# Half of the memory tokens loaded into free activation tiles behind the first key weight, and the delta rule's masked ratios made by VectorE

## The chip, the cores and the metric

The kernel runs on one core of a Trainium2 chip. The metric is the time of one execution on the device in microseconds: 2902.29 us, the median of three runs (2901.53 to 2903.21).

## The reference

One layer of a streaming encoder on 512 tokens of width 2048, in float32. The input is normalised and projected by one matrix; its columns feed a gated delta rule (8 heads of 128) and an RWKV-7 mixer (16 heads of 64). Their outputs are projected and added, then follow cross attention into 256 memory tokens, a squared-ReLU MLP and a last norm.

```python
h  = x
y  = rmsnorm(h, norm_mix) @ w_in                       # 512 x 2048 by 2048 x ~7500
h += concat[GDN(y_gdn), RWKV7(y_rwkv)] @ w_out
mn = rmsnorm(mem, norm_mem)                            # 256 memory tokens
k, v = mn @ wk, mn @ wv ; q = rmsnorm(h, norm_xattn) @ wq
h += softmax(q k^T / sqrt(512)) v @ wo                 # 4 heads of 512
h += square(relu(rmsnorm(h, norm_mlp) @ w_up)) @ w_down
out = rmsnorm(h, norm_final)
```

In the delta rule a chunk's matrix is masked by position and scaled by the ratio of decays:

```python
gamma = where(i >= j, exp(G[i] - G[j]), 0)
M     = where(i > j, (beta k)_i . k_j * gamma, 0)      # solved as (M + I) X = rhs
```

## The kernel before

Activations lie with the width on the 128 partitions, so the input is 16 tiles of 128 x 512. A float32 product is made of two-part numbers: `split_` writes a rounded high half on ScalarE (`whi`, `xhi`) and the rest on VectorE (`wlo`, `xlo`), and TensorE adds high by high, low by high and high by low. A projection block of 128 output columns (`py`) takes 16 x 3 matmuls of 128 x 512; its weight comes as two halves of 128 x 1024 (512 KB). There are 59 such blocks (NIN), the stage of the first 911 us.

Between these matmuls stands the work of the mixers. Per head pair j the function `rwkv` and per head h the function `gdn` form small matrices, whose 16 x 16 diagonal blocks are inverted by `inverse_blocks` on GpSimd (tiles `sr` for RWKV, `sgi`, `sgj` for the delta rule): the matrix is stored to DRAM (`ndri`, `ndgi`), read back as blocks, inverted in some thirty small operations, stored again (`bg16T`, `bg8T` and so on) and read into the tiles `r`, `E`, `gk`, `gqn`. `inverse_levels` then joins the blocks by matmuls (`ri7x`, `ri7w`, `ri7u`, and `gi7x` and so on; the digit is the pair or head). In `gdn` the norm of the keys is a sum of squares over partitions, done as a matmul (`gn`, inputs `sumh`, `suml`), and the products of keys are `pkk`. The tile `gE` holds the ratios gamma, `gEs` the same with the strict mask and a minus sign.

Behind the projections come the key stage and the query stage: `kp` multiplies the memory by the key weights, `kq` multiplies the keys by the query weights. In `kp` a weight half serves 8 matmuls of 128 x 512 (high half of the weight against both halves of the memory, side by side in a tile `mhl`) and 8 of 128 x 256. The order of halves is (block 0, first half), (1, first), (0, second), (1, second), then block by block.

The order of the work is not that of the code. Each function is a generator (a chain) that yields one operation at a time; `run` takes, again and again, the chain whose next operation can start first by the planner's own account (`start`, `cost`: fixed prices for each engine and 2.9 us and more for a DMA's landing), with a rank added. The operation is then recorded in `issue`, so that nearly all rows of the profile have its line, 256. Engines run what they were given in order, and so does the queue of DMA issues on SyncE (SP): a DMA that waits holds all behind it. The planner knows an engine's speed alone, nothing of two engines in each other's way. A chain also waits inside the planner for its turn: an operation for a busy GpSimd holds the chain's later operations back until the plan's clock has come to it.

`loader` works off the list `wq` of loads through three buffers (`wraw`), each taken when the buffer's last content was split: weights ("w"), and the memory in four parts of 512 KB, once for its sums of squares ("s") and once for its values ("m"). `memory` splits a part into four tiles `mhl`, which lie in the places (tag "act", 32 tiles) of the input tiles `xhi`, `xlo`; it waits until the last projection has used them (events "x"). `presums`, low in rank, fills free time with sums of blocks of the down projection (tiles `ds`, stored as `sd`). The later stages (`vp`, `vo`, output and MLP) use the same places again.

Of the kernel before, what the change touches and what calls it, by code (L numbers as in the profile page):

```python
# [17 lines left out]
P = 128  # L18
T = 512
M = 256  # L20
# [53 lines left out]
def build(tc, I, out):  # L74
# [23 lines left out]
    def col(name, i=0):  # L98
        o, w = PRM[name]
        return prm[:, o + i:o + i + 1]  # L100
# [92 lines left out]
    class Lane:  # L193
# [6 lines left out]
        def __getattr__(self, nm):  # L200
# [3 lines left out]
                return self.key, nm, getattr(self.eng, nm), a, k, out, aps, self.slack  # L204
            return op

    SL, SM = Lane(nc.sync, "SP", wait=6000.0), Lane(nc.sync, "SP", margin=8000.0)
    DV, AC, GS, TE, SY = (Lane(e, k) for e, k in ((V, "DVE"), (S, "ACT"), (GP, "POOL"), (PE, "PE"), (nc.sync, "SP")))

# [136 lines left out]
        yield TE.matmul(pt, which, hi, start=False, stop=True)  # L346
        lock.pop()

    def act_tile(nm, dt=F32R):
        return tile_of(pa, [P, 512], dt, "act", nm, 32)  # L350

    mixd = [pd.tile([P, T], F32, name=f"mixd{i}", tag=f"mixd{i}") for i in range(16)]
    KQd = [pd.tile([P, 1024], F32, name=f"kqd{i}", tag=f"kqd{i}") for i in range(16)]
# [58 lines left out]
                yield from presum(e, m, c, min(c + width, 2048), d, Lane(nc.sync, "SP", margin=5000.0), Lane(nc.sync, "SP", 0.0, 0.0))  # L412

    hk = [("w", I["wk"][n][:, h * 1024:(h + 1) * 1024]) for n, h in kpo]
    wq += [("m", m) for m in mem4[:3]] + hk[:1] + [("m", mem4[3])] + hk[1:]
    wq += [("w", I["wqT"][n][:, g * 1024:(g + 1) * 1024]) for n in range(KD) for g in range(2)]
    NKP, NKQ = 2 * NIN, 2 * NIN + 2 * KD
    raws, halves, used, whole, piece = {}, {}, set(), set(), {}
# [12 lines left out]
    def loader():  # L431
        w = nm = 0
        for i, (kind, _) in enumerate(wq):
            yield lambda: i in raws
            if kind == "w":
                if w in (2, 3):
                    hi, lo = (tile_of(pm, [P, 1024], F32R, t, f"w{t}", 1) for t in ("BK", "AR", "GA", "GB")[2 * w - 4:2 * w - 2])
                else:
                    prev = (w if w < 2 else w - 2) - NWS
                    if prev >= 0:  # L440
                        yield lambda: prev + 2 * (prev > 1) in used
                    hi, lo = halves[w] if w in piece else wsplit()
                if w in piece:
                    yield after("piece", w)
                    yield from split_(raws[i][:, 512:], hi[:, 512:], lo[:, 512:])
                else:
                    yield from split_(raws[i], hi, lo)
                    halves[w] = hi, lo
                whole.add(w)
                w += 1  # L450
            else:
                yield from (memory if kind == "m" else squares)(nm % 4, raws[i])
                nm += 1
            if NWR < i + NWR <= 2 * NWR:
                chain(late(i + NWR), 2)
            elif i + NWR < len(wq):
                yield rawload(i + NWR)
# [29 lines left out]

    def xin():
        for k in range(KD):
            hi, lo = act_tile(f"xhi{k}"), act_tile(f"xlo{k}")  # L490
            yield from split_(xr[k], hi, lo, col("norm_mix", k))
            xhi.append(hi)
            xlo.append(lo)
            if k + XA < KD:
                yield xload(k + XA)
# [70 lines left out]
    def projections():  # L566
        pts = [psb(f"py{n}") for n in range(2)]
        yield from gemm_(pts, xhi, xlo, 0)
        for n in range(2):
            chain(evict(n, pts[n]), 0)  # L570
        for n in range(2, NIN):
            if n == NSQ[3] + 3:
                yield after("macc")
                pt = psb("pms", "mm", 2)
                mc = ybuf[macc[0]]
                yield TE.matmul(pt[:, 0:M], ones, mc[:, 0:M], start=True, stop=False)
                yield TE.matmul(pt[:, 0:M], ones, mc[:, M:2 * M], start=False, stop=True)
                chain(memnorm(pt, mc[:, M:2 * M]), 1)
            if n >= 4:
                yield after("py", n - 2)  # L580
            pt = psb(f"py{n}", "mm", 2)
            yield from gemm_([pt], xhi, xlo, 2 * n, left="x" if n == NIN - 1 else None)
            chain(evict(n, pt), 0)
        yield after("py", NIN - 2)
        kpt = {}
        for i, (n, h) in enumerate(kpo):
            if h == 0:
                yield after("kp", n - 2) if n >= 2 else after("py", NIN - 1)
                kpt[n] = psb(f"kp{n}", "mm", 2)
            pt = kpt[n]  # L590
            yield half(NKP + i)
            wh, wl = halves[NKP + i]
            for part in (0, 1) if h == 0 else (1, 0):
                for k in range(8 * h, 8 * h + 8):
                    yield lambda: len(mhl) > k
                    if part == 0:
                        yield TE.matmul(pt, wh[:, k % 8 * P:k % 8 * P + P], mhl[k], start=k == 0, stop=k == KD - 1)
                    else:
                        yield TE.matmul(pt[:, 0:M], wl[:, k % 8 * P:k % 8 * P + P], mhl[k][:, 0:M], start=False, stop=False)
            used.add(NKP + i)  # L600
            if h == 0:
                continue
            t = act_tile(f"khl{n}")
            khl.append(t)
            chain(kevict(n, pt, t[:, 0:M], t[:, M:2 * M]), 0)
        for i in range(2 * KD):
            n, g = i // 2, i % 2
            if i == 0:
                yield after("inverted", 7)
            yield after("kp", KD - 2 + i) if i < 2 else after("kq", i - 2)  # L610
            yield half(NKQ + i)
            wh, wl = halves[NKQ + i]
            pts = [psb(f"kq{n}_{g}_{hh}", ("mm", "mg")[hh], 2) for hh in range(2)]
            for z in range(8):
                yield TE.matmul(pts[z // 4], wh[:, z * P:z * P + P], khl[g * 8 + z], start=z % 4 == 0, stop=False)
            for z in range(8):
                yield TE.matmul(pts[z // 4][:, 0:M], wl[:, z * P:z * P + P], khl[g * 8 + z][:, 0:M],
                                start=False, stop=z % 4 == 3)
            used.add(NKQ + i)
            chain(qevict(i, pts), 0)  # L620
# [463 lines left out]
    def gdn(h):  # L1084
# [45 lines left out]
            yield DV.scalar_tensor_tensor(out=E[:, cs], in0=E[:, cs], scalar=RT[:, c, 0, h:h + 1],  # L1130
                                          in1=K("mbias"), op0=ALU.subtract, op1=ALU.min)
        yield AC.activation(E, E, AF.Exp)
        Es = tl("gEs")
        yield GS.tensor_tensor(out=c3(Es), in0=c3(E), in1=K("sneg").unsqueeze(1).broadcast_to([P, 4, P]), op=ALU.mult)
        kn = yield from normed(k_, None, "gkn", 0)
        kb = tl("gk")
        yield DV.tensor_tensor(out=kb, in0=kn, in1=B, op=ALU.mult)
# [1 line left out]
        for c in range(4):  # L1139
            cs = slice(c * P, (c + 1) * P)  # L1140
            yield TE.matmul(pkk[:, cs], kn[:, cs], kb[:, cs], start=True, stop=True)
        NTm = Es
        yield DV.tensor_tensor(out=NTm, in0=pkk, in1=Es, op=ALU.mult)

        def store(full):
            yield SY.dma_start(full[:, 0:4, :], c3(NTm)[hA, :, 0:64])
# [83 lines left out]
            chain(gdn(h + 1), 3)  # L1230


    mhl = []
    mrs = rstd[:, 0:M]
    macc = []

# [15 lines left out]
    def memory(k4, raw):  # L1252
        for i in range(4):
            k = 4 * k4 + i
            yield after("x", k // 2)
            t = act_tile(f"mhl{k}")
            yield from split_(raw[:, i * M:(i + 1) * M], t[:, 0:M], t[:, M:2 * M], col("norm_mem", k))
            mhl.append(t)

    def memnorm(pt, mw):  # L1260
        yield from rsq_(mw, pt[:, 0:M], 1.0 / 2048, b_eps6)
# [23 lines left out]
    chain(pieces(), 1)  # L1285
    chain(consts(), 3)
    chain(loader(), 2)
    chain(xin(), 1)
    chain(xsum(), 4, ("rstd",))
    chain(derived(), 3, ("derived",))  # L1290
# [1149 lines left out]
```

## Time and profile before

| what | value |
|---|---|
| median of three runs | 2902.29 us |
| the profiled execution: its time, its span | 2902.95 us, 2901.2 us |
| TensorE (PE) busy | 2868.0 us, 99% |
| VectorE (DVE), ScalarE (ACT) busy | 2333.1 us, 1569.9 us |
| GpSimd (POOL) busy | 227.0 us, all of it in the first 14 of 40 slices |
| moved by DMA | 553.01 MB, 191 GB/s on average |

A row of the timeline is start, duration, engine, line, operation, output<-inputs and tile sizes; in brackets stands the engine's idle time ahead of the row and what ended it. SPq rows are DMA issues. A row of the waits gives the waiting engine and tile, whom it waited for, the total, the number of times and the longest. Matmuls are pipelined: from one start to the next is the time that counts, the duration of one is longer. A granted clock (PEclk) of 1.00 is full speed.

### The profile page before, as it was taken

The page shows a single profiled execution, that of the slowest core. Times are in us where ns is not written, and L with a number is a line of the kernel's source. Part 1 is how long each engine was busy: PE and PEld are TensorE (multiplying, and loading weights), DVE is VectorE, ACT ScalarE, POOL GpSimd, SP SyncE. Part 2 cuts the span into 40 slices and gives each one's busy share as a digit, 9 for nine tenths or more (in the row PEclk, how much of TensorE's full clock was granted, in tenths as well). Part 3 has the DMA queues.
Part 4 walks back from the last instruction along what each step waited for, and adds up shares of the span by engine and source line. Part 5 has one row for each costly group of instructions (what it writes and reads, how often), then busy time and mean ns, then how long its engine had stood idle before and what let it go on. Part 6 is the DMA issues. An engine that isn't in the chain of part 4 may idle for free.

```text
span 2901.2 us, 49161 instructions
## 1 busy us (share of the span) xinstructions
PE 2868.0 (99%) x18794; PEld 2420.4 (83%) x18794; DVE 2333.1 (80%) x3551; ACT 1569.9 (54%) x2233; POOL 227.0 (8%) x547
## 2 busy tenths in 40 slices
PE   8999999999999999999999999999999999999998
PEld 7877877777777888879988888888888888888887
DVE  7787787787887876769956898899998878787888
ACT  6454555545655555564444656555555645454544
POOL 0213213223122100000000000000000000000000
PEclk9999999999999999999999999999999999999999
DMA  5657556556656688684423344656665878978733
GB/s 190 175 143 184 160 160 173 161 154 185 173 154 198 199 256 276 229 286 159 125 94 94 106 157 158 196 194 203 187 201 181 291 243 278 296 256 273 267 102 109
DMA packets 320924, 553.01 MB, mean 191 GB/s; under 512 B 101096, under 2 KB 188396, under 8 KB 320688
## 3 DMA queue, kind: packets, MB, share of 16 engines
q1 hardware_dynamic: 293296, 518.41, 57.9%
q10 hardware_dynamic: 27392, 31.46, 3.1%
q8 instruction: 147, 2.41, 0.3%
q14 instruction: 89, 0.73, 0.1%
HBM read 443.45 MB, written 106.31 MB: 189 GB/s over the span
## 4 chain that ended last, share of the span: by engine, by line
PE 93%; DMA 2%; DVE 2%; ACT 1%; issue 1%; ACTq 0%; SPq 0%; DVEq 0%
PE py L256 22%; PE mxu L256 12%; PE mgd L256 6%; PE mgu L256 6%; PE mxd L256 6%; PE op L122 5%; PE vp L122 3%; PE mmu L256 3%; PE sc L122 3%; PE at L122 3%; PE mmd L256 3%; PE scrd L256 3%; PE scgd L256 3%; PE kq L256 3%; PE kp L256 3%; PE vo L122 1%
## 5 line engine op out<-in xcount | busy, mean ns | idle before, releaser
L256 ACT CAST whi<-wraw 128x1024 fp32r<-128x1024 f32 (+1 forms) x366 | 383.4, 1048 | 364.2 <-PE py L256 150.4
L256 DVE TENSOR_TENSOR wlo<-wraw,whi 128x1024 fp32r<-128x1024 f32 (+1 forms) x366 | 450.5, 1231 | 101.0 <-ACT whi L256 92.2
L256 PE MATMUL py<-xhi,whi 128*128 128x512 f32 x928 | 372.6, 401 | 8.1 <-ACT xhi L256 8.1
L256 PE MATMUL py<-xhi,wlo 128*128 128x512 f32 x928 | 372.8, 402 | 0.0
L256 PE MATMUL py<-xlo,whi 128*128 128x512 f32 x928 | 372.7, 402 | 0.0
L256 ACT CAST whi<-w 128x1024 fp32r<-128x1024 f32 x176 | 185.3, 1053 | 170.3 <-PE mxd L256 35.2
L256 DVE TENSOR_TENSOR wlo<-w,whi 128x1024 fp32r<-128x1024 f32 x176 | 214.8, 1221 | 44.4 <-ACT whi L256 41.1
L256 PE MATMUL mxu<-cb,whi 128*128 128x512 f32 x1016 | 249.3, 392 | 0.0
L256 PEld LDWEIGHTS mxu<-cb,whi 128*128 128x128 f32 x1016 | 184.7, 189 | 34.3
L256 PEld LDWEIGHTS py<-xhi,whi 128*128 128x128 f32 x928 | 175.0, 189 | 42.6 <-ACT xhi L256 8.1
L256 PEld LDWEIGHTS py<-xhi,wlo 128*128 128x128 f32 x928 | 175.0, 189 | 35.5 <-issue 1.8
L256 PEld LDWEIGHTS py<-xlo,whi 128*128 128x128 f32 x928 | 174.9, 189 | 34.8 <-DVE xlo L256 0.5
L131 DVE TENSOR_TENSOR wlo<-wraw,whi 128x1024 fp32r<-128x1024 f32 x112 | 136.6, 1221 | 44.0 <-ACT whi L130 43.5
L130 ACT CAST whi<-wraw 128x1024 fp32r<-128x1024 f32 x112 | 117.6, 1051 | 85.9 <-PE op L122 29.4
L256 PE MATMUL mxu<-cb,wlo 128*128 128x256 f32 x1016 | 142.7, 283 | 0.7 <-DVE wlo L256 0.7
L256 PEld LDWEIGHTS mxu<-cb,wlo 128*128 128x128 f32 x1016 | 135.1, 191 | 6.0 <-DVE wlo L256 0.9
L256 ACT ACT_TABLE_LOAD x87 | 111.6, 1283 | 36.4 <-DVE suml_gn L256 16.5
L256 PE MATMUL mgu<-cb,whi 128*128 128x512 f32 x512 | 129.3, 394 | 0.1
L256 PE MATMUL mxd<-whi,cb 128*128 128x512 f32 x512 | 126.7, 389 | 0.7 <-DVE acc L256 0.7
L256 PE MATMUL mgd<-whi,cb 128*128 128x512 f32 x512 | 126.4, 389 | 0.0
L256 ACT CAST whi<-ws 128x1024 fp32r<-128x1024 f32 x75 | 79.0, 1053 | 72.3 <-PE mgu L256 48.2
L122 PE MATMUL op<-ob,whi 128*128 128x256 f32 (+1 forms) x752 | 115.3, 304 | 0.1
(945 smaller groups left out, 6447.2 us busy)
## 6 DMA issues: line engine op xcount, KB each, us to landing
wraw<-in_w_in SPq DMA_DIRECT2D x116, 512.0 KB, 4.6
wraw<-in_w_up SPq DMA_DIRECT2D x65, 512.0 KB, 3.6
w<-in_w_up SPq DMA_DIRECT2D x63, 512.0 KB, 4.0
ds<-in_w_dm SPq DMA_DIRECT2D x128, 205.0 KB, 4.1
sd_s<-ds SPq DMA_DIRECT2D x128, 205.0 KB, 4.7
wraw<-sd_s SPq DMA_DIRECT2D x51, 512.0 KB, 4.9
w<-sd_s SPq DMA_DIRECT2D x50, 512.0 KB, 5.5
w<-in_w_dm SPq DMA_DIRECT2D x48, 512.0 KB, 5.0
```

The costliest lines, as they stand in the source:

```text
L122: PE.matmul(o, l, r, start=start, stop=stop, skip_group_check=again)
L130: S.copy(hi, src)
L131: V.tensor_tensor(out=lo, in0=src, in1=hi.bitcast(F32), op=ALU.subtract)
L256: f(*a, **k)
```

## The change

Two things are changed, and with them the planner's order wherever it bears on them.

The memory's values. The list of loads now begins the key stage with the first key weight, then two of the four memory parts, then the other weights. The other two parts no longer go through the three buffers: the new chain `straight` loads them as four tiles `mraw` of 128 x 512 into the places of the input tiles 4 and 5, as soon as the last projection has used these, and `placed` splits them from there. For that the 32 places are kept as two groups, 28 ("act") and 4 ("acr"); later tiles take the small one where the count of tiles, in groups of four, is at group 7, 11, 19, 27 or 35. The event "direct" starts `placed` when the first two parts are at their last tile. `mhl` becomes a dictionary, and a kp matmul waits for its own tile.

The masked ratios. The product of `gE` with the mask is taken from GpSimd, where it stood ahead of the norm of the keys in the chain, and given to VectorE, behind the products of keys and right ahead of the operation that uses it.

```diff
+    SD = Lane(nc.sync, "SP", 0.0, 1500.0)
...
-    def act_tile(nm, dt=F32R):
-        return tile_of(pa, [P, 512], dt, "act", nm, 32)
+    acts = [0]
+
+    def act_tile(nm, dt=F32R, x=None):
+        few = x in (4, 5)
+        if x is None:
+            few = acts[0] // 4 in (7, 11, 19, 27, 35)
+            acts[0] += 1
+        return tile_of(pa, [P, 512], dt, "acr" if few else "act", nm, 4 if few else 28)
...
-    wq += [("m", m) for m in mem4[:3]] + hk[:1] + [("m", mem4[3])] + hk[1:]
+    wq += hk[:1] + [("m", m) for m in mem4[:2]] + hk[1:]
...
-                yield from (memory if kind == "m" else squares)(nm % 4, raws[i])
+                yield from (memory if nm >= 4 else squares)(nm % 4, raws[i])
...
-            hi, lo = act_tile(f"xhi{k}"), act_tile(f"xlo{k}")
+            hi, lo = act_tile(f"xhi{k}", x=k), act_tile(f"xlo{k}", x=k)
...
-                    yield lambda: len(mhl) > k
+                    yield lambda: k in mhl
...
-        Es = tl("gEs")
-        yield GS.tensor_tensor(out=c3(Es), in0=c3(E), in1=K("sneg").unsqueeze(1).broadcast_to([P, 4, P]), op=ALU.mult)
...
-        NTm = Es
-        yield DV.tensor_tensor(out=NTm, in0=pkk, in1=Es, op=ALU.mult)
+        NTm = tl("gEs")
+        yield DV.tensor_tensor(out=c3(NTm), in0=c3(E), in1=K("sneg").unsqueeze(1).broadcast_to([P, 4, P]), op=ALU.mult)
+        yield DV.tensor_tensor(out=NTm, in0=pkk, in1=NTm, op=ALU.mult)
...
+            if k == 7:
+                events.add(("direct",))
             yield from split_(raw[:, i * M:(i + 1) * M], t[:, 0:M], t[:, M:2 * M], col("norm_mem", k))
-            mhl.append(t)
+            mhl[k] = t
+
+    def straight():
+        for j in range(4):
+            yield after("x", 4 + j // 2)
+            t = tile_of(pa, [P, 512], F32, "acr", f"mraw{j}", 4)
+            yield SD.dma_start(t.rearrange("p (a b) -> p a b", b=M), mem4[2 + j // 2][:, j % 2 * 2:j % 2 * 2 + 2, :])
+            direct[j] = t
+
+    def placed():
+        yield after("direct")
+        for k in range(8, KD):
+            yield lambda: (k - 8) // 2 in direct and ("x", k // 2 + 2) in events
+            t, raw = act_tile(f"mhl{k}"), direct[(k - 8) // 2][:, k % 2 * M:k % 2 * M + M]
+            yield from split_(raw, t[:, 0:M], t[:, M:2 * M], col("norm_mem", k))
+            mhl[k] = t
...
+    chain(straight(), 1)
+    chain(placed(), 2)
```

The DMA queue SP at the end of the projections, before, from the store of the last RWKV inverse on (`in_wk` are key weights, `in_memT` the memory, `lg` a gate weight, `sd` and `ds` the sums of the down projection):

```order
L256 DMA bg16T<-sr_10077 64x16x16
L256 DMA bg16U<-sr_10077 64x16x16
L256 DMA lg_10354<-in_g2a 128x128
L256 DMA lg_10354<-in_g2b 32x128 x3
L256 DMA r_10299<-bg16T 64x8x64 x2
L256 DMA E_558_10300<-bg16U 64x4x64 x4
L256 DMA wraw_10395<-in_wk 128x1024
L256 DMA sd_1_s_154<-ds_55_829 128x410
L256 DMA sd_1_s_156<-ds_54_828 128x410
L256 DMA wraw_10444<-in_memT 128x1024
L256 DMA sd_1_s_155<-ds_53_827 128x410
L256 DMA wraw_10475<-in_wk 128x1024
```

The same place in the changed kernel:

```order
L257 DMA bg16T<-sr_10099 64x16x16
L257 DMA bg16U<-sr_10099 64x16x16
L257 DMA wraw_10354<-in_memT 128x1024
L257 DMA r_10357<-bg16T 64x8x64 x2
L257 DMA E_564_10358<-bg16U 64x4x64 x4
L257 DMA mraw_10417<-in_memT 128x512
L257 DMA mraw_10425<-in_memT 128x512
L257 DMA mraw_10428<-in_memT 128x512
L257 DMA mraw_10434<-in_memT 128x512
L257 DMA wraw_10402<-in_wk 128x1024
L257 DMA sd_1_s_154<-ds_55_829 128x410
L257 DMA sd_1_s_156<-ds_54_828 128x410
```

Before, the first key weight is the first load behind the reads of the inverse, and three memory parts went out ahead of the rows shown. Now the key weight shown is the second; the first stands 15 rows ahead of bg16T, right behind the read of the inverse's blocks (sr), with one memory part after it, and the second memory part and the four direct loads stand here. The read sr, which followed two stores (ndri), four loads ds, a store mixd and a memory part, follows the two stores and one ds.

TensorE in the key stage, before, where the first level of the last RWKV inverse ends (ri7u) and the second begins:

```order
L256 MATMUL ri7s_10530<-k_10406,E_558_10300 64x64 x2
L256 MATMUL ri7t_10531<-k_10406,E_558_10300 64x64 x2
L256 MATMUL ri7u_10529<-E_558_10300,k_10406 64x64 x16
L256 MATMUL ri7x_10592<-r_10299,GA_9996 64x64
L256 MATMUL ri7x_10592<-r_10299,GB_9997 64x64
L256 MATMUL ri7w_10593<-r_10299,GA_9996 64x64
```

And now:

```order
L257 MATMUL ri7s_10581<-k_10419,E_564_10358 64x64 x2
L257 MATMUL ri7t_10582<-k_10419,E_564_10358 64x64 x2
L257 MATMUL ri7u_10580<-E_564_10358,k_10419 64x64 x16
L257 MATMUL kp_10562<-mhl_10459,wlo_10507 128x256
L257 MATMUL kp_10562<-mhl_10464,wlo_10507 128x256
L257 MATMUL kp_10562<-mhl_10469,wlo_10507 128x256
```

Where the second level followed at once, 23 kp matmuls stand between, and one more ahead of pkk behind it. Ahead of the first level stand the last projection matmuls and 4 kp (before: the sum gn, which has moved into the projections, and 6 kp); between its ri7w and ri7s stand 21 kp instead of 10.

GpSimd before, at the end of an RWKV inverse in the fourth head (sr) and the start of a delta-rule inverse (sgi):

```order
L256 TENSOR_TENSOR sr_4934<-sr_4934,sr_4935 64x15
L256 COPY sr_4934<-sr_4934 64x256
L256 TENSOR_TENSOR gEs_5218<-gE_4369,cst 128x512
L256 MEMSET sgi_5328 32x256
L256 MEMSET sgi_5328 32x16
```

VectorE in the changed kernel, in the same head:

```order
L257 TENSOR_TENSOR wlo_5188<-wraw_4906,whi_5187 128x1024
L257 TENSOR_TENSOR gk_5200<-gkn_5175,gqd_4951 128x512
L257 TENSOR_TENSOR gEs_5227<-gE_4208,cst 128x512
L257 TENSOR_TENSOR gEs_5227<-pkk_5219,gEs_5227 128x512
L257 SCALAR_TENSOR_TENSOR gq_5233<-y_182,prm,gq_5233 128x512 x3
```

The mask's product has left GpSimd, whose order is otherwise the same, and stands on VectorE directly ahead of the product with pkk.

2 lines of the change are left out of this document (1 added, 1 removed).

## The prediction

> **What bounds the kernel now.** I read the page's busy times first, then the list of waits on PE, then PE in order of time where those waits fall, with the granted clock.
>
> ```profile
> span 2901.2 us, 49161 instructions
> PE 2868.0 (99%) x18794; PEld 2420.4 (83%) x18794; DVE 2333.1 (80%) x3551; ACT 1569.9 (54%) x2233; POOL 227.0 (8%) x547
> ...
> PE py L256 <- ACT xhi L256: 8.1, 1, 8.1
> PE kp L256 <- ACT whi L256: 4.4, 1, 4.4
> PE gn L256 <- DVE suml_gn L256: 2.6, 4, 0.7
> PE vp L122 <- DVE y L256: 1.5, 1, 1.5
> ...
> PE pu L256 <- DVE E L256: 0.7, 1, 0.7
> PE pkk L256 <- DVE gk L256: 0.6, 1, 0.6
> ...
> PE ri7w L256 <- DVE E L256: 0.5, 1, 0.5
> ...
> PE pov L256 <- DVE k L256: 0.2, 1, 0.2
> ```
>
> PE is busy for 99% of the span, so the change can win only what PE loses by waiting, and it issues the same matmuls as before. The start (8.1) isn't touched. The two large entries left are the ones that the change is near: 4.4 us at the first key matmul (kp, waiting for the high half of its weight) and four waits of the sums of squares (gn, waiting for VectorE).
>
> ```profile
> 911.07 0.40 PE L256 MATMUL gn<-sumh_gn,onesr 128*128 128x512 f32 x1
> 915.85 2.58 PE L256 MATMUL kp<-mhl,whi 128*128 128x512 f32 x6 [4.38 <-ACT whi L256]
> ...
> core 0: us, PE busy (x) PEld busy (x) DVE busy (x) ACT busy (x) POOL busy (x), PEclk, DMA share, GB/s
> 911.40:915.85 4.45, 0.07 (x2) 0.01 (x1) 0.35 (x2) 1.10 (x2) 0.00 (x0) 1.00 0.92 292
> 915.85:919.25 3.40, 3.40 (x38) 2.42 (x38) 1.70 (x2) 3.37 (x7) 0.00 (x0) 0.56 0.91 315
> ...
> 1126.10:1129.50 3.40, 3.21 (x19) 2.87 (x20) 2.36 (x5) 2.06 (x4) 0.00 (x0) 1.00 0.70 199
> ```
>
> The wait costs more than its 4.38: the 3.40 us behind it ran at a granted clock of 0.56, while the 1.5 us wait of vp (at 1126) left the clock at 1.00.
>
> Why the weight is late is read on the DMA queue and ScalarE:
>
> ```profile
> 902.12 0.58 SPq L256 DMA_DIRECT2D bg16T<-sr  x1
> ...
> 905.70 1.27 SPq L256 DMA_DIRECT2D r<-bg16T  x2
> 907.02 2.61 SPq L256 DMA_DIRECT2D E<-bg16U  x4
> 909.73 0.55 SPq L256 DMA_DIRECT2D wraw<-in_wk  x1
> 910.37 0.85 SPq L256 DMA_DIRECT2D sd_s<-ds  x2
> 911.32 0.40 SPq L256 DMA_DIRECT2D wraw<-in_memT  x1
> ...
> 914.75 1.04 ACT L256 CAST whi<-wraw 128x1024 fp32r<-128x1024 f32 x1 [5.80 <-DMA wraw<-in_wk]
> ```
>
> SP issues in order. The key weight stood behind the store and the reads of the last RWKV inverse (bg16T, r, E) and went out at 909.73; ScalarE had it 5.0 us later, and 1.1 us after that PE went on (915.85).
>
> The four gn waits have another cause. One of them:
>
> ```profile
> 457.52 0.62 POOL L256 COPY sr<-sr 64x256 f32<-64x256 f32 x1
> 458.47 1.91 POOL L256 TENSOR_TENSOR gEs<-gE,cst 128x512 f32<-128x512 f32 x1 [0.33 <-ACT gE L256]
> ...
> 459.15 1.67 DVE L256 TENSOR_TENSOR ds<-ds,ds 128x410 f32<-128x410 f32 x1
> 460.75 0.68 DVE L256 TENSOR_TENSOR suml_gn<-sg,sumh_gn 128x512 fp32r<-128x512 f32 x1
> ...
> 454.80 0.39 PE L256 MATMUL py<-xhi,whi 128*128 128x512 f32 x1
> ...
> 460.46 0.39 PE L256 MATMUL py<-xlo,whi 128*128 128x512 f32 x1
> 461.48 0.50 PE L256 MATMUL gn<-suml_gn,onesr 128*128 128x512 f32 x1 [0.62 <-DVE suml_gn L256]
> ...
> 569.93 2.73 DVE L256 TENSOR_TENSOR wlo<-wraw,whi 128x1024 fp32r<-128x1024 f32 x1 [1.98 <-ACT whi L256]
> ...
> L256 POOL TENSOR_TENSOR gEs<-gE,cst 128x512 f32<-128x512 f32 x8 | 11.1, 1386 | 2.2 <-ACT gE L256 2.2
> ...
> L256 DVE TENSOR_TENSOR wlo<-wraw,whi 128x1024 fp32r<-128x1024 f32 x364 | 449.1, 1234 | 101.0 <-ACT whi L256 92.2 <-PE py L256 5.2 <-PE kp L256 1.3
> L256 DVE TENSOR_TENSOR ds<-ds,ds 128x410 f32<-128x410 f32 x128 | 75.9, 593 | 1.6
> ```
>
> While GpSimd makes the masked ratios gEs, the VectorE operation beside it is held: 1.67 us in place of a mean 0.59 here, 2.73 in place of 1.23 a head later. The sum behind it is late by that, and PE waits. This is the very operation that the change takes from GpSimd.
>
> **The change part by part.** Terms are against the profiled execution (span 2901.2, time 2902.95), 0.7 above the median 2902.29.
>
> Masked ratios, moved to VectorE. PE steps from 454.80 to 460.46 are 25, 0.226 each; the step into gn took 1.02, so a gn wait costs 0.79, and four cost 3.2. With the GpSimd operation gone, the ds row ends 1.08 earlier and the sum is ready before its matmul's turn: **−3.2**; bounds 0 (the plan moves as well and a sum stands close behind something else) and −3.2. VectorE gains eight operations, for which the nearest row is the product behind each, of the same shape:
>
> ```profile
> L256 DVE TENSOR_TENSOR gEs<-pkk,gEs 128x512 f32<-128x512 f32 x8 | 5.5, 690 | 10.3 <-PE pkk L256 10.3
> ```
>
> 8 × 0.69 = 5.5 us, against 1.08 + 1.50 = 2.6 of stretching in the two heads shown. VectorE idled 101 us ahead of its weight splits alone, and the new operation delays only the product and the store to the inverse behind it; PE reaches the inverse's first use some 30 us of matmuls later (matmuls counted in the order). I take 0 on PE, bounds 0 and +5.5 (if every one lay on PE's path). If that cover is gone, the head's first inverse matmul (gi x) is late next.
>
> [...]
>
> The first key weight ahead of the memory. It is loaded right behind the inverse's read (sr), 15 DMA rows ahead of bg16T, and its split stands ahead of the memory's on ScalarE and VectorE. The wait of 915.85 − 911.07 − 0.23 = 4.55 goes: **−4.6**. The clock loss goes with it: 3.40 × (1 − 0.56) = **−1.5**.
>
> What is late next is the second key weight. The projections ended at about 910.8 (911.07 less a step); call it P. The second half of the memory's first two parts and the four direct loads now stand on SP between bg16U and that weight. bg16T at 902.12 is P − 8.7. The two stores at 0.58 and the memory load at 0.40 leave SP free near 904, and the loads lg that followed the stores are ahead of them now, so the reads r start between 904 and 905.7 (as before), and r and E take 1.27 + 2.61 with gaps, to between 908 and 909.6. Four direct loads at 0.40 make it P − 1.3 to P + 0.4. Add the 5.0 and 1.1 of the first weight: ready at P + 4.8 to P + 6.5. PE comes to it after 16 kp matmuls and the ri7x block:
>
> ```profile
> 984.72 12.29 PE kp L256 x69
> ...
> wraw<-in_wk SPq DMA_DIRECT2D x16, 512.0 KB, 3.9
> ```
>
> 16 × 0.178 = 2.85, and about 1.0 for ri7x: P + 3.9, so it would wait 0.9 to 2.6. The inverse's read (sr) now goes out ahead of five DMAs that it followed before, which may bring bg16T and all behind it up to 2.0 us forward (five issues at 0.40); then the wait is 0 to 0.6. I take **+1.0**, nearer the lower end since the weight's median landing is 3.9 and not 5.0; bounds 0 and +6.1 (the whole old wait and its clock loss). The third weight, 1.7 later on SP for four stores at half of 0.85, is needed 2.85 and the next inverse block later: covered.
>
> The four small waits behind it (pu, pkk, ri7w, pov: 0.7 + 0.6 + 0.5 + 0.2 = 2.0). ri7w waited for E on VectorE:
>
> ```profile
> 920.20 1.66 DVE L256 SCALAR_TENSOR_TENSOR mhl<-wraw,prm,mhl 128x256 fp32r<-128x256 f32 x4
> ...
> 922.80 0.69 DVE L256 TENSOR_TENSOR E<-E,ri7u 128x512 f32<-128x512 f32 x1 [0.19 <-PE ri7u L256]
> ```
>
> The last memory part, loaded last at 911.32, stood in its way. In the changed order 23 kp matmuls (4.1 us) lie between ri7u and the next ri7x and ri7w, where none did; pkk comes behind them too, so that its input gk is ready by then; and 26 instead of 23 and 12 instead of 8 kp matmuls lie ahead of pov and pu: **−2.0**, bounds 0 and −2.0.
>
> Memory bytes stay (two loads of 512 KB become four of 256 KB). The later stages keep their order but for a few lines, taken at 0; a piece of the down-projection sums moves ahead, under PE.
>
> Sum: −3.2 − 4.6 − 1.5 − 2.0 + 1.0 = −10.3. 2902.95 − 10.3 = 2892.6 for the execution, **2892.0** against the median.
>
> **The rivals.**
> - *The key weights wait again.* The change moves the wait from the first weight to the second or third, behind the direct loads. For it: the DMA share was 0.92 there, and SP is in order. Against it: PE now has 2.85 us of kp to do first. Giving back half to all of 4.6 + 1.5: 2895 to 2898; named 2896.
> - *Only the head of the key stage gains.* The sums stay late because the plan moves them closer, or a GpSimd piece holds VectorE there: −3.2 is lost, 2895.2. For it: four of eight heads, not all, waited before, so the places shift.
> - *Slower: SP waits for GpSimd with projection weights behind it.* In each head the store of the inverse (bg8T) holds SP until GpSimd is done, and the heads' chains now come earlier on it.
>
> ```profile
> SPq L256 <- POOL sgi L256: 36.1, 10, 8.2
> ```
>
>   It held SP 8.2 us at most and PE didn't notice, since three buffers of 24 matmuls each (5.4 us) are ahead. If the hold passes that cover by 2.3 us in seven heads, 16 us are lost and the sum turns to +5.8: 2908. Against it: the GpSimd operation that stood in front of each inverse is gone.
> - *No change.* The first weight is loaded early but split late: its split needs the buffer of the third last projection half, which is used up 48 matmuls, 10.9 us, ahead of P, and then 1.04 + 1.23 do. It would take 8 us of other work on ScalarE in front of it to bring the wait back whole; with the sums also unchanged, 2901.
>
> [...]
>
> **How the numbers follow.** Forecast 0.60, first rival 0.16, second 0.08, slower 0.09, no change 0.07. A change of 0.2%, 5.8 us, is about what a measurement here can tell from none: faster means below 2896.5. The forecast, the second rival and a third of the first are faster: 0.60 + 0.08 + 0.05 = 0.73, and slower is 0.09 of the slow rival; the rest, 0.18, is the same. The forecast's own range is 2889 to 2894.5: all terms with no new wait give −11.3, and small waits like pkk's elsewhere could add 2. For 8 in 10 the range reaches to the first rival's end: 2888.5 to 2898.5.
>
> **What would show it.** Right: no gn wait of 0.6 or more, kp's wait for ScalarE under 1.5 us, the clock at 1.00 behind it, VectorE up by some 3 us net, GpSimd down by 11, ds and wlo back to 0.59 and 1.23 everywhere beside it. Wrong: a kp wait above 3 us with a clock below 1, or py waiting for whi.

## The result, and the profile after

The changed kernel takes 2896.64 us, the median of 21 runs (2892.45 to 2902.86), against 2901.53 us (2899.13 to 2904.81, 21 runs) before: a ratio of 0.9984, with a 95% interval of 0.9978 to 0.9990. It is faster by 4.9 us. That is the forecast's sign, about half of its 10.3 us, and 0.16%, which lies inside the 0.2% that the prediction had called hard to tell from no change, though the interval leaves no change out. 2896.64 lies above the forecast's own 2889 to 2894.5 and inside the wider 2888.5 to 2898.5. All executions reported here were fast ones but one, of 11392 us, of the fourth kernel below; no figure contains it.

The profiled execution of the changed kernel is the slowest of its 21, with 2902.86 us. An experiment below ran the kernel again, with a profile of 2896.66 us. Both are used here, called the first and the second profile. The table splits their time on TensorE. P is the end of the projections, that is the start of the last py matmul plus its step of 0.23; the other bounds are the first starts of pA (the gate products of the first RWKV pair), kq and op, and the start of the last matmul. Before, two gn matmuls (0.5 us) stand behind P, which the changed order has in the heads.

| stretch, us | before (2902.95) | changed, first (2902.86) | changed, second (2896.66) | forecast |
|---|---|---|---|---|
| start to first pA | 58.78 | 59.54 | 58.60 | as before |
| heads: pA to P | 852.04 | 853.55 | 847.60 | -3.2 |
| key stage: P to first kq | 120.44 | 118.20 | 117.18 | -7.1 |
| first kq to first op | 273.66 | 273.66 | 275.48 | as before |
| op to the last matmul | 1586.43 | 1586.27 | 1586.14 | as before |

So the key stage won 2.2 to 3.3 us in place of 7.1 (-4.6 - 1.5 - 2.0 + 1.0), and the heads won 4.4 in one profile and lost 1.5 in the other.

The page of the changed kernel, first profile, answers as follows to the rows shown of before: busy times, then the waits of PE.

```profile
span 2901.1 us, 49179 instructions
PE 2866.7 (99%) x18794; PEld 2422.2 (83%) x18794; DVE 2333.5 (80%) x3559; ACT 1572.1 (54%) x2233; POOL 218.0 (8%) x539
...
PE rs L257 <- DVE BK L257: 2.0, 1, 2.0
PE kp L257 <- ACT whi L257: 1.9, 1, 1.9
PE kp L257 <- DVE wlo L257: 1.4, 2, 0.7
...
PE pwt L257 <- issue: 1.2, 1, 1.2
PE gs L257 <- DVE TtG L257: 1.2, 1, 1.2
...
PE ri7s L257 <- DVE k L257: 1.0, 1, 1.0
PE gi7w L257 <- DVE gv L257: 0.9, 1, 0.9
PE ri6s L257 <- DVE k L257: 0.8, 1, 0.8
```

The four gn waits are gone, and so are the 4.4 of kp and, in the key stage, the small waits of pu, pkk, ri7w and pov. In their place stands a longer list of others. GpSimd fell by 9.0 us and VectorE rose by 0.4 net, where 11 and 3 were forecast. The groups of VectorE in the same profile show the prices:

```profile
L257 DVE TENSOR_TENSOR gEs<-gE,cst 128x512 f32<-128x512 f32 x8 | 5.5, 687 | 0.0
L257 DVE TENSOR_TENSOR gEs<-pkk,gEs 128x512 f32<-128x512 f32 x8 | 5.5, 691 | 4.6 <-PE pkk L257 4.5
...
L257 DVE TENSOR_TENSOR wlo<-wraw,whi 128x1024 fp32r<-128x1024 f32 x364 | 445.5, 1225 | 93.1 <-ACT whi L257 87.3 <-PE py L257 1.6 <-DMA sl<-in_w_dm 1.5
L257 DVE TENSOR_TENSOR ds<-ds,ds 128x410 f32<-128x410 f32 x128 | 75.7, 591 | 6.4 <-DMA ds<-in_w_dm 5.0
```

The new operation takes 0.69, as taken from its neighbour. The split wlo fell by 3.6 us in sum. New is what VectorE stands for in front of ds: 6.4 us against 1.6 before, 5.0 of it for the load of such a piece.

In the second profile, PE at the key stage, and the granted clock there:

```profile
908.86 1.11 PE L257 MATMUL kp<-mhl,wlo 128*128 128x256 f32 x8
912.53 0.80 PE L257 MATMUL kp<-mhl,whi 128*128 128x512 f32 x1 [2.57 <-ACT whi L257]
```

```profile
909.09:912.50 3.41, 0.88 (x8) 0.67 (x6) 0.00 (x0) 1.06 (x2) 0.00 (x0) 1.00 1.08 312
912.50:915.92 3.42, 3.39 (x8) 2.72 (x9) 3.41 (x7) 2.33 (x6) 0.00 (x0) 0.50 0.85 307
```

The first key weight is in time, the second is not: 2.57 us of waiting, and half the clock for the window behind it, just what the first weight had cost before, only shorter. (In the first profile the wait is 1.9 us and the clock stays at 1.00.) The queue of DMA issues and ScalarE in the first profile show why:

```profile
901.64 0.58 SPq L257 DMA_DIRECT2D bg16T<-sr  x1
...
905.03 1.27 SPq L257 DMA_DIRECT2D r<-bg16T  x2
906.40 2.56 SPq L257 DMA_DIRECT2D E<-bg16U  x4
909.00 2.02 SPq L257 DMA_DIRECT2D mraw<-in_memT  x4
911.12 0.38 SPq L257 DMA_DIRECT2D wraw<-in_wk  x1
```

```profile
917.64 1.04 ACT L257 CAST whi<-wraw 128x1024 fp32r<-128x1024 f32 x1 [4.22 <-DMA wraw<-in_wk]
```

With P at 913.10 there, the weight goes out at P - 2.0 and ScalarE has it 6.5 us later, at P + 4.5. The prediction had P - 1.3 to P + 0.4 and 5.0 us. In the second profile it is P - 2.5 and 7.7 us. So the weight left somewhat earlier than forecast and landed later, and PE went on with it at P + 5.6 and P + 6.3, inside the forecast P + 4.8 to P + 6.5.

### The profile page after: what moved, and what is told of

The parts are those of the page before. It is cut to its first block, busy times and chain, and to the rows that moved or that the text cites. A ratio compares the mean times of both kernels' runs of the same rounds, so it can differ in the third digit from the quotient of the medians.

```text
span 2901.1 us, 49179 instructions
## 1 busy us (share of the span) xinstructions
PE 2866.7 (99%) x18794; PEld 2422.2 (83%) x18794; DVE 2333.5 (80%) x3559; ACT 1572.1 (54%) x2233; POOL 218.0 (8%) x539
## 4 chain that ended last, share of the span: by engine, by line
PE 92%; DMA 3%; DVE 2%; ACT 1%; POOL 1%; issue 1%; SPq 0%; ACTq 0%; DVEq 0%; POOLq 0%
PE py L257 21%; PE mxu L257 12%; PE mgd L257 6%; PE mxd L257 6%; PE mgu L257 6%; PE op L122 6%; PE vp L122 3%; PE sc L122 3%; PE at L122 3%; PE mmd L257 3%; PE mmu L257 3%; PE scrd L257 3%; PE scgd L257 3%; PE kq L257 3%; PE kp L257 2%; DMA wraw<-in_wo 1%
## 5 line engine op out<-in xcount | busy, mean ns | idle before, releaser
L257 PE MATMUL mgd<-whi,cb 128*128 128x512 f32 x512 | 126.4, 389 | 0.0
```

Source lines behind the costliest of these rows:

```text
L257: f(*a, **k)
```

## The experiments

The part of the heads that was lost in the first profile (853.55 against 847.60) has a place, too. VectorE, and PE next to it, in that profile:

```profile
816.44 0.59 DVE L257 TENSOR_TENSOR ds<-ds,ds 128x410 f32<-128x410 f32 x1 [4.14 <-DMA ds<-in_w_dm]
817.85 0.67 DVE L257 TENSOR_TENSOR ds<-ds,ds 128x410 f32<-128x410 f32 x1 [0.82 <-DMA ds<-in_w_dm]
```

```profile
821.02 0.43 PE L257 MATMUL rs<-BK,BTz 128*128 128x64 f32 x2 [2.04 <-DVE BK L257]
...
822.83 0.45 PE L257 MATMUL rs<-Qs,WTz 128*128 128x64 f32 x1 [0.70 <-DVE Qs L257]
```

A piece of the down-projection sums, which is there to fill free time, stands at the head of VectorE's order before its load has landed, and everything behind it is late. In the 14 profiles of this study VectorE stands there, from 812 to 821 us, in all eight kernels and repetitions whose planner has the ratios on VectorE and the pieces as before (2.1 to 4.1 us), and in none of the four that keep the old plan of the ratios, so the hold came with the ratios and not with the memory. From here came the first three theories, which the first four kernels were to tell apart: the two halves of the change simply add up (1); the gn waits are won, but the new order puts other waits in the heads (2); all of the gain is in the key stage (3).

### The ratios alone

```diff
-        Es = tl("gEs")
-        yield GS.tensor_tensor(out=c3(Es), in0=c3(E), in1=K("sneg")..., op=ALU.mult)
...
+        NTm = tl("gEs")
+        yield DV.tensor_tensor(out=c3(NTm), in0=c3(E), in1=K("sneg")..., op=ALU.mult)
```

> The kernel before with the masked ratios on VectorE and nothing else: the memory tokens and the first key weight are loaded as before. Theory 1 (the two halves of the change add up; the ratio half is worth the four gn waits): no gn wait of 0.6 us or more, kp still waits 4.4 us with the clock at about 0.56 behind it, time 3.2 us shorter (2898). Theory 2 (the gn waits are gone, but the new plan puts other waits of some 2 to 4 us in the heads): no gn wait, but new waits of VectorE's results elsewhere, time within 1 us of before. Theory 3 (all the gain is in the key stage): the same as theory 2 in time, but with gn waits still there.

Measured: 2894.93 us, 0.9981 (0.9972 to 0.9990), 5.7 us shorter than before. That is more than any theory gave it, and it is shorter than the whole change. The surprise is in the key stage, where this kernel loads everything in the old order:

```profile
894.50 0.58 SPq L256 DMA_DIRECT2D bg16T<-sr  x1
...
897.01 1.27 SPq L256 DMA_DIRECT2D r<-bg16T  x2
898.38 2.56 SPq L256 DMA_DIRECT2D E<-bg16U  x4
900.98 0.60 SPq L256 DMA_DIRECT2D wraw<-in_wk  x1
```

P is 905.99 here, so the first key weight goes out at P - 5.0, and not at P - 1.1 as before. PE waits 0.6 us for it (1.4 in a repetition below) and the clock stays at 1.00 from 890 to 935 us. The new plan, made without the ratios on GpSimd, has the read of the last inverse's blocks (sr) ahead of loads that it followed before, and the loads lg ahead of bg16T, with no edit to the loads at all.

### The memory half alone

The same two operations are put back into the changed kernel, with the ratio on GpSimd.

> The changed kernel with the masked ratios put back on GpSimd: only the memory's second half is loaded into activation places and the first key weight goes ahead. Theory 1: some gn waits of 0.6 to 0.8 us each are back, kp's first wait is gone, the second key weight is waited for by about 2 us; 4.6 + 1.5 + 2.0 - 2.0 = 6.1 us shorter than before (2896). Theory 2: the new plan costs some 2 us here too: 4 us shorter. Rival (the key weights wait again): the second or third key weight takes back 3 to 6 us, time within 2 us of before.

Measured: 2905.24 us, 1.0016 (1.0007 to 1.0024), 4.6 us longer than before. The first key weight is in time, the four gn waits are there (2.6 us), and the key stage takes 126.4 us against 120.4. PE and ScalarE in it:

```profile
925.06 0.79 PE L257 MATMUL kp<-mhl,wlo 128*128 128x256 f32 x2 [1.99 <-ACT mhl L257]
931.85 0.98 PE L257 MATMUL kp<-mhl,wlo 128*128 128x256 f32 x2 [6.00 <-ACT mhl L257]
```

```profile
923.55 1.04 ACT L257 CAST whi<-wraw 128x1024 fp32r<-128x1024 f32 x1 [2.13 <-DMA wraw<-in_wk]
924.51 0.91 ACT L257 ACTIVATE mhl<-mraw,prm 128x256 fp32r<-128x256 f32 x2
930.34 1.04 ACT L257 CAST whi<-wraw 128x1024 fp32r<-128x1024 f32 x1 [4.93 <-DMA wraw<-in_wk]
931.29 0.91 ACT L257 ACTIVATE mhl<-mraw,prm 128x256 fp32r<-128x256 f32 x2
```

The memory's second half (mraw) was issued from 908.43 to 910.40. Its splits stand in ScalarE's order behind the cast of a key weight that is still on its way, and follow that cast without any wait of their own, so PE waits for memory that only lacks its turn. No theory had this; the rival in the expectation came nearest, by another path than the one it named.

### The changed kernel again, and later pieces

> The changed kernel once more, unaltered, for a second profile of it and its time beside the others on one chip: 4 to 6 us shorter than before. If the 4.1 us in which VectorE stood for a load of the down-projection pieces at 816 us of the first profile (and the 6.8 us of halved clock behind it) belong to the plan, they are there again. If they belong to that one execution, the span is 3 to 6 us shorter than the 2901.1 us of that profile and neither is seen; the key stage shows a wait of about 1.9 us for the second key weight in both cases.

Measured: 2896.66 us, 0.9985 (0.9976 to 0.9994). VectorE stood again at the same place, for 3.38 us, but had both parts of the piece at once, and PE waited 0.7 us there where it had waited 2.7, with the clock at 0.50 behind it for 6.83 us. So the hold belongs to the plan; what it costs differs from execution to execution, which fits the wide spread of the changed kernel (10.4 us, against 5.7 before).

The fourth kernel was to take the hold away.

```diff
-    ... Lane(nc.sync, "SP", margin=5000.0), Lane(nc.sync, "SP", 0.0, 0.0))
+    ... Lane(nc.sync, "SP", margin=8000.0), Lane(nc.sync, "SP", 0.0, 0.0))
```

> The changed kernel with the planner told that a load of a down-projection piece lands 3 us later, so that the subtractions on such pieces stand further back in VectorE's order. Theory 2 (VectorE is held by loads of these pieces that land after its turn comes): VectorE's idle time in front of ds falls, the waits of rs, gs and BK's readers get shorter, and the time is 2 to 4 us shorter than the changed kernel's. Theory 1 (these holds cost nothing as a rule): within 1.5 us of the changed kernel.

Measured: 2935.87 us, the median of three executions, 1.0120 (1.0105 to 1.0136). Every theory missed this by nearly 40 us. With later pieces fewer of them are done in the heads (132 subtractions up to 920 us, against 148): the sums left over move to the end, where PE waits 12.0 us at once for a weight that is read from them, and the heads and the key stage take 10.6 and 11.5 us more than in the second profile. The edit changed far more than the place it was aimed at, so it says nothing on what the hold costs.

### What moved the time: contention, or the plan

Two kernels are to separate the two things that moving an operation does. The first keeps every order as before and changes the executing engine only, so that VectorE carries eight operations its plan did not count; the second keeps the changed kernel's order and adds GpSimd's work again.

```diff
-        yield GS.tensor_tensor(out=c3(Es), in0=c3(E), ...)
+        yield Lane(V, "POOL").tensor_tensor(out=c3(Es), in0=c3(E), ...)
```

> The kernel before, where VectorE executes the masked ratios while the planner still counts them as GpSimd's: every engine's order stays as before, but for the eight operations that stand on VectorE now. Contention theory (GpSimd's operation stretched the one beside it on VectorE, and that made the four gn waits): the gn waits are gone, kp still waits 4.4 us with the clock halved behind it, 3.2 us shorter than before. Plan theory (what the ratios alone won, 5.7 us, came from the order that the planner made without them on GpSimd): within 1 us of before. Both can hold in part: 3.2 from contention and 2.5 from the plan.

Measured: 2901.00 us, 0.9998 (0.9989 to 1.0007): nothing. In the profile one gn wait of 0.5 us is left, as the contention theory says. But a new wait of 1.1 us for a read of the inverse (gi4x) stands in the heads, so that these are 1.3 us shorter and not 3.2, and the first key weight does not come sooner because PE does:

```profile
915.50 2.93 PE L256 MATMUL kp<-mhl,whi 128*128 128x512 f32 x6 [4.89 <-ACT whi L256]
```

The wait is 0.5 us longer than before and ends within 0.35 us of where it did (915.85), and the six matmuls behind it take 2.93 us against 2.58 before.

```diff
         yield AC.activation(E, E, AF.Exp)
+        NTm = tl("gEs")
+        GP.tensor_tensor(out=c3(NTm), in0=c3(E), in1=K("sneg")..., op=ALU.mult)
```

> The changed kernel with the eight GpSimd operations added again at their old place, unknown to the planner; their result is overwritten by VectorE's. Orders are otherwise those of the changed kernel. Contention theory: the operations beside them on VectorE stretch by 1 to 1.5 us in most heads, several gn waits of 0.6 to 0.8 us are back, 2 to 4 us longer than the changed kernel. Plan theory: the stretched operations are off the path in this order, within 1 us of the changed kernel.

Measured: 2901.12 us, 1.0001 (0.9992 to 1.0010), 4.5 us longer than the changed kernel: a little more than the contention theory's 2 to 4. Six gn waits are back. So is a wait of 2.2 us for a read of an RWKV inverse (ri6x, 0.4 in the first profile), with the clock at 0.50 from 806.85 to 810.27: GpSimd, which makes that inverse, has more to do as well, so the 4.5 us need not be VectorE's contention alone. GpSimd and VectorE in the head at 334 us, and the wait of PE that belongs to them:

```profile
334.33 1.65 POOL L1141 TENSOR_TENSOR gEs<-gE,cst 128x512 f32<-128x512 f32 x1
```

```profile
334.12 2.30 DVE L257 TENSOR_TENSOR ds<-ds,ds 128x410 f32<-128x410 f32 x2
336.35 0.78 DVE L257 TENSOR_TENSOR suml_gn<-sg,sumh_gn 128x512 fp32r<-128x512 f32 x1
```

```profile
PE gn L257 <- DVE suml_gn L257: 3.8, 6, 0.7
```

The two ds operations there take 2.30 us. In the first profile, without the GpSimd operations, the mean of one is 0.59, so two make 1.18.

So in these kernels neither thing wins anything alone: the new plan with the contention takes 2901.1 (the memory half in it; without it this was not run), the old plan without contention 2901.0, new plan and no contention 2895 to 2897.

### Three places for one wait

```diff
         for j in range(4):
-            yield after("x", 4 + j // 2)
+            yield lambda: ("x", 4 + j // 2) in events and ("raw", K1 + 0) in events
```

K1 is the second key weight's number in the list of loads; the event says that its load is out.

> The changed kernel with the four direct loads of the memory's second half behind the second key weight on SP instead of ahead of it. If the second key weight is late because these four loads stand ahead of it (2.0 us of SP and 1 MB): its wait of 1.9 to 2.6 us is gone, and with it the halved clock that followed in one profile: 2 to 4 us shorter than the changed kernel. If it is late because of the traffic at that place, whatever the order, or if the memory's second half is then late in its turn: within 1 us, or longer.

Measured: 2897.04 us, 0.9988 (0.9979 to 0.9997), within 1 us of the changed kernel. Its profile is of the slowest of its 11 executions (2905.25), so what these waits cost as a rule is not shown. The second weight's wait is gone, and two others have its place, for the low half of the third weight and for the memory's second half:

```profile
918.65 0.98 PE L257 MATMUL kp<-mhl,wlo 128*128 128x256 f32 x6 [1.48 <-DVE wlo L257]
921.78 0.98 PE L257 MATMUL kp<-mhl,wlo 128*128 128x256 f32 x2 [2.15 <-ACT mhl L257]
```

```diff
-        yield SY.dma_start(D, blk)
+        yield (Lane(nc.sync, "SP", wait=-3000.0) if nm == "ri7" else SY).dma_start(D, blk)
```

> The kernel before with one thing moved: the read of the last RWKV inverse's blocks (sr) stands on SP right behind the two stores that it needs, ahead of four loads of down-projection pieces, a store and a memory load that it followed before. Read theory (the first key weight was late because this read landed 6.4 us after its issue behind those bytes, in place of 3.0 with the ratios on VectorE alone, and held GpSimd's inverse, its store and all of SP behind it): kp's first wait falls from 4.4 to about 1 us, the clock stays at 1.00 behind it, 4 to 5 us shorter than before; the gn waits stay. Rival (the first key weight is late because of its own place on SP): kp's wait stays above 3 us and the time within 1 us of before.

Measured: 2906.94 us, 1.0021 (1.0012 to 1.0030), longer. The read landed in 3.1 us, and bg16T went out 4.2 us sooner than before. But then three pieces' loads, gqd and lg went ahead, and the key weight left at 909.76, as late as before:

```profile
897.90 0.58 SPq L256 DMA_DIRECT2D bg16T<-sr  x1
...
899.25 2.38 SPq L256 DMA_DIRECT2D ds<-in_w_dm  x3
...
909.76 0.37 SPq L256 DMA_DIRECT2D wraw<-in_wk  x1
```

kp waited 3.6 us, and the last delta-rule inverse (gi7) some 6 more. The read theory falls as a single cause: the late read was only the first of the things in front of the weight.

### Without the memory half, other load orders

> The ratios alone on VectorE once more, beside the variants of this call. If the memory half of the change wins nothing once the ratios are moved: again 5 to 6 us shorter than before, 1 to 2 us shorter than the changed kernel's 2896.6. If the first measurement of it was lucky: 4 us or less.

Measured: 2895.17 us, 0.9981 (0.9972 to 0.9990), 5.8 us shorter than before. Both measurements of the ratios alone have a mean of 2895.3 (22 runs), all of the changed kernel's one of 2896.9 (32 runs): a difference of 1.6 us, with a 95% interval of 0.5 to 2.7 by resampling the runs. These come from several sessions; the two kernels measured side by side in one differ by 1.2 us in their means (-0.5 to 3.0). With the ratios moved, the memory half wins nothing, and costs some 1 to 2 us if anything.

```diff
-    wq += [("m", m) for m in mem4[:3]] + hk[:1] + [("m", mem4[3])] + hk[1:]
+    wq += [("m", m) for m in mem4[:2]] + hk[:2] + [("m", m) for m in mem4[2:]] + hk[2:]
```

> The ratios alone on VectorE, with the load order at the key stage as it is needed: the memory's first half, the first two key weights, the memory's second half, the other key weights; no direct loads. Order theory (what is needed first must be loaded first): the first kp wait of 0.6, the second of 1.4 and the wait of ri7s for VectorE behind the memory's splits (1.5) go, 2 to 3 us shorter than the ratios alone. Supply theory (the stage waits for the sum of its loads, with the DMA engines 0.92 to 0.98 busy from 900 to 915 us, whatever their order): the memory's second half is waited for in turn, within 1 us of the ratios alone, or longer.

Measured: 2893.59 us, 0.9976 (0.9966 to 0.9985): 7.4 us shorter than before and the fastest kernel of the study, though the 1.2 us of its mean to the ratios alone are within the spread (95%: 2.5 shorter to 0.2 longer). No kp matmul waits any more, and the key stage takes 114.3 us. What PE waits for there are the inverse's matmuls, ri7s and ri7x, both for VectorE behind the memory's splits:

```profile
PE ri7s L256 <- DVE k L256: 1.4, 1, 1.4
PE ri7x L256 <- DVE r L256: 1.4, 1, 1.4
```

```diff
-    wq += [("m", m) for m in mem4[:3]] + hk[:1] + [("m", mem4[3])] + hk[1:]
+    wq += [("m", m) for m in mem4[:2]] + hk[:1] + [("m", m) for m in mem4[2:3]] + hk[1:2] + [("m", mem4[3])] + hk[2:]
```

> The ratios alone on VectorE, with the load order first half of the memory, first key weight, third quarter, second key weight, fourth quarter: only the first key weight and the third quarter change places, and the second weight and the fourth. Order theory: 1 to 2 us shorter than the ratios alone. Supply theory: within 1 us of them.

Measured: 2897.08 us, 0.9990 (0.9981 to 0.9999), 1.9 us longer than the ratios alone: both theories missed. The first two weights are in time, the third is not, and ScalarE has it behind the splits of the last memory part. That looks like the pattern of the memory half alone, but both loads are late: the cast, too, stands 0.15 us for its own load.

```profile
914.48 1.70 ACT L256 ACTIVATE mhl<-wraw,prm 128x256 fp32r<-128x256 f32 x4 [4.69 <-DMA wraw<-in_memT]
916.34 1.04 ACT L256 CAST whi<-wraw 128x1024 fp32r<-128x1024 f32 x1 [0.15 <-DMA wraw<-in_wk]
```

```profile
918.69 1.65 PE L256 MATMUL kp<-mhl,wlo 128*128 128x256 f32 x6 [4.50 <-DVE wlo L256]
```

Up to the third weight the supply theory holds for three orders: PE begins with it at P + 12.8 here, at P + 12.9 where two weights go first (its cast ends at P + 11.5 in both), and at P + 12.5 in the changed kernel's second profile. With the ratios alone it is P + 14.7, in both measurements, so there a better order does bring it 2 us forward. From there to kq it takes 101.5 us in the kernel with two weights first, 104.8 here, 104.7 in the changed kernel, and 103.3 and 102.4 with the ratios alone. The lead on the kernel of this part lies there: of its 3.3 us, 1.2 are two waits that it does not have, for wlo near 985 us (0.7 here) and for gi7 (0.5); the rest was not traced. Both profiles are of the fastest execution of their kernel. Why this order is spared these two waits was not tested.

```diff
-    ... Lane(nc.sync, "SP", margin=5000.0), Lane(nc.sync, "SP", 0.0, 0.0))
+    ... Lane(nc.sync, "SP", wait=1500.0, margin=5000.0), Lane(nc.sync, "SP", 0.0, 0.0))
```

> The ratios alone on VectorE, with the planner told to put each load of a down-projection piece 1.5 us later than the store that frees its place allows. Hold theory (SP stands in its order before such loads, 3.5 us at 904 us of the profile, with the second key weight behind them): the second key weight goes out earlier, and VectorE's wait for a piece at 809 us (3.7 us) falls; 1 to 3 us shorter than the ratios alone. Rival (the plan moves and other waits come): within 1 us, or longer by what the pieces that are left over cost at the end.

Measured: 2924.36 us, 1.0082 (1.0068 to 1.0096). The pieces now hold VectorE for longer, not shorter, in three heads out of eight:

```profile
735.98 0.59 DVE L256 TENSOR_TENSOR ds<-ds,ds 128x410 f32<-128x410 f32 x1 [7.89 <-DMA ds<-in_w_dm]
```

```profile
PE rs L256 <- DVE BK L256: 18.0, 3, 6.6
```

Like the fourth kernel it was meant to weaken the hold, and did not. It did show what a hold costs when it meets PE: 18.0 us in three waits.

## Why the prediction was half right

**Masked ratios, -3.2: right in mechanism, and more came with it.** The gn waits went, and they come back when GpSimd's operations do (six, 3.8 us). In the second profile the heads won 4.4. The steps into the four gn matmuls give 3.2 of it, as forecast, but the steps into four new waits (pwt twice, ri6s and rs, 1.5 us of waiting) take 2.3 back. Eight fewer changes of matmul shape (652 to 644) make some 2.0, by medians of each pair of shapes before (0.32 us from a 128x512 matmul to a 64x64, 0.23 between two of 128x512); the prediction had not counted these. The remaining 1.5 was not traced. The eight new operations take 0.69 each, and no first inverse matmul (gi x), which the prediction named as late next, waits in either profile. No ds or wlo of the heads is as long as the stretched ones before: in the first profile the longest ds is 0.83 us and the longest wlo 1.59 (before: 1.67 and 2.73).

**First key weight, -4.6 and -1.5: the wait went, but it was not the list that was needed for it, and its worth did not stay.** The step that failed is the attribution: the prediction gave the whole wait to the place of that load in the list. The memory half alone does clear it, but the ratios alone, with the list as it was, leave 0.6 us of it (1.4 in the repetition), the first with a clock of 1.00, as SP comes to the weight at P - 5.0 instead of P - 1.1. So these 6.1 us were booked for a half of the change that, once the ratios are moved, wins nothing. That the time still fell inside the wider range is luck in part: the ratio half won 5.7 in place of 3.2, and made up for part of it.

**What is late next, +1.0: mis-sized.** The second key weight was named, it left SP 0.7 and 1.2 us ahead of the forecast's early bound, and the bounds 0 to 6.1 held it. It cost 1.9 and 2.6 us of waiting, in the second profile with a window at 0.50 behind it. The lower end was taken because of the weight's median landing of 3.9 us; ScalarE had it after 6.5 and 7.7, with a DMA share of 0.86 from its issue to its cast in the first profile, and in the second of 0.77 from 905 to 910 us and 0.95 from 910 to 915. The prediction had clock lost behind it in the upper bound alone: before, 4.38 us of waiting had a lower clock behind it and 1.5 us had not; here 2.57 us had 0.50 behind it, and 1.9 us had 1.00.

**Four small waits, -2.0: gone and replaced.** pu, pkk, ri7w and pov are gone from the key stage. ri7s (1.0), kp for wlo (1.4 in two), pwt (1.2), gs (1.2) and gi7w (0.9) stand there now in the first profile, 5.7 us in sum. The prediction looked at the four and at none that might come.

**Later stages and other heads, 0: failed.** The order was said to keep but for a few lines. The hold of VectorE in front of ds, which was not there before, cost PE 2.7 us and a clock of 0.50 for 6.83 us in the first profile, and 0.7 us in the second. From kq to op, the second profile is 1.8 us longer than before and the first is not, so that is the execution and not the order.

Of the rivals, "the key weights wait again" (2896) came nearest in time and in what it describes; it was given 0.16. In the kernel of the memory half alone, which is 4.6 us slower than before, it is memory and not a weight that PE waits for.

Open: why the plan of the memory half alone puts its splits behind the casts was not traced through the planner, what the hold of VectorE costs by itself was not isolated, as both edits against it moved the whole plan, and the new plan with contention but without the memory half was not run.

## What to carry to other kernels

Where a planner makes the order, an edit is two edits: what it does to the engines, and what it does to everyone's place. Run each half of a change alone, and once with the order frozen; here two halves looked like -3.2 and -7.1 and were -5.7 and, behind it, no gain (+1.2 to +1.6). In the changed kernel the first key weight went first, and PE waited 1.9 and 2.6 us for the second. In the kernel of the memory half alone ScalarE stood 4.93 us for the load of a weight, with splits of the memory behind it that then had no wait of their own, so read the order of the splits as closely as that of the loads.

## What the runs showed of the hardware

Up to the last matmul, the profile before has the granted clock at 0.50 once, for 3.41 us from 916.26, and the first profile of the changed kernel once, for 6.83 us from 822.56. In the 3.41 us ahead of these PE was busy for 0.41 and 1.11 us. In the second profile it was 0.88 us ahead of the 0.50 at 912.50, and with GpSimd's operations added 1.65 ahead of the 0.50 at 806.85. Before, the windows of 3.41 us from 909.44 and from 1124.48 had PE busy for 2.02 and 1.91 us, and the clock behind them was 1.00. Two more such windows, from the variant that loads two weights first and from the ratios alone, each with the window behind it:

```profile
916.03:919.44 3.41, 1.76 (x38) 1.15 (x36) 3.41 (x8) 2.84 (x4) 0.00 (x0) 1.00 0.46 173
919.44:922.85 3.41, 3.41 (x12) 3.12 (x13) 2.44 (x4) 1.04 (x1) 0.00 (x0) 0.50 0.66 211
```

```profile
910.13:913.54 3.41, 1.88 (x63) 1.53 (x64) 2.74 (x7) 0.96 (x3) 0.00 (x0) 1.00 0.96 259
913.54:916.96 3.42, 2.30 (x24) 1.91 (x19) 0.93 (x1) 1.21 (x2) 0.00 (x0) 1.00 0.95 378
```

Behind 1.76 us busy the clock was 0.50, behind 1.88 us it was 1.00. In the second profile PE was busy for 3.39 us of the 3.42 at 0.50, and the next window was at 1.00. In the first profile it was busy for 3.14 us of the first window at 0.50, with a wait of 0.70 us (rs) that ended in it at 822.83, and the next, busy throughout, was at 0.50 too; the one from 829.39 was at 1.00. How the clock goes at other shares of busy time, these rows do not show.
